# Two up projections computed by Strassen's seven products

## The chip, the cores and the metric

One core of one Trainium2 chip runs the kernel. The metric is device microseconds for one execution. TensorE (PE) multiplies, with its weight loads counted apart (PEld); VectorE (DVE) and ScalarE (ACT) do the elementwise work; SyncE's queue (SP) issues the transfers from HBM.

## The reference

Two residual blocks work on 512 tokens of width 1024, in float32. The first is two layers deep, the second one layer. What the change touches are the parts with the large weight matrices:

```
# first block, twice
proj = u @ w_in[l]                     # 1024 x 5444, then attention, convolution, gates
x = x + merged @ w_mix_out[l]
u = rmsnorm(x, norm_mlp[l])
x = x + square(relu(u @ w_mlp_up[l])) @ w_mlp_down[l]     # 1024 -> 4096 -> 1024
# second block, once
mod = silu(c) @ w_ada + b_ada          # shifts, scales and gates, 1024 x 6144
h = modulate(rms_norm(x, g_ffn), sh_f, sc_f)
x = x + gt_f * ((silu(h @ w_gate) * (h @ w_up)) @ w_down) # 1024 -> 2816 -> 1024
```

## The kernel before

Activations stand transposed: a tile holds 128 features by 512 tokens, so `x` is eight tiles. A product takes a 128x128 piece of the weights as the stationary operand and streams 512 tokens. To keep float32 accuracy with TensorE's rounded float32 type, each operand is split into a high part and a low part (`split` for weights, L171 on ScalarE and L172 on VectorE; `hilo` for activations, L285 and L286), and three matmuls stand for one: high x high, high x low, low x high (L230 to L232 in `linear`). `gateup` has a loop of its own for the FFN (L1315 to L1317).

Weights come in chunks of 1 MB (L161, three buffers). A chunk is cut into units of 4 k-tiles by 256 columns, and each unit is split when the order of work reaches two units ahead of it; four buffers hold split units. The order of work is a list of items that `Prog.run` goes through: a "unit" makes the splits that are due and runs as many background pieces as the rate allows, a "do" emits instructions. A scheduler then orders each engine's queue and places the tiles; a tile of the common pool (60 tiles of 128x512) is free again after its last reader.

In an MLP layer the hidden 4096 features are worked in four groups of 1024. `up` makes eight hidden tiles of one group, four at a time, over eight k-tiles. `evup` evacuates each from PSUM: scale and relu on VectorE (L732), square on ScalarE (L733), then `hilo`. `down` multiplies the group's hidden tiles into all eight output tiles, and `evdn` adds each to `x` (L740). The groups stand one behind the other: up 0, up 1, down 0, up 2, down 1, and so on. In layer 1 the background pieces are `ada`: the 1024 x 6144 matrix is multiplied by a vector on VectorE (L803), 48 steps of two, each with two loads of its own, at 0.8 steps a unit.

The FFN does the same with a pair of matrices: `gateup` makes two gate tiles and two up tiles, applies silu on ScalarE (L1323), multiplies them (L1326) and splits the result (L1330, L1331); `evff` adds the down tiles to `x` (L1345). Where a stage waits for a norm, `parts_=2` runs the tokens in two halves, with matmuls of 256 columns.

Of the kernel before, what the change touches and what calls it, by code (L numbers as in the profile page):

```python
# [17 lines left out]
D = 1024  # L18
NT = T // P
# [6 lines left out]
FF2 = 2816  # L26

# [13 lines left out]
K_RES = 1408  # L41
# [6 lines left out]
class Prog:  # L48


    def __init__(self, split, ahead):
        self.items = []
        self.split = split
        self.ahead = ahead

    def run(self):
        units = [p for k, p in self.items if k == "unit"]
        nxt = 0
# [4 lines left out]
        for kind, pay in self.items:  # L63
            if kind == "unit":
                while nxt < len(units) and nxt <= cur + self.ahead:
                    self.split(units[nxt])
                    nxt += 1
# [32 lines left out]

@with_exitstack
def blocks_kernel(ctx: ExitStack, tc: tile.TileContext, a: dict, out: bass.AP, stop=None):
# [5 lines left out]
    gp = ctx.enter_context(tc.tile_pool(name="gp", bufs=60))  # L108
    bp = ctx.enter_context(tc.tile_pool(name="bp", bufs=1))
    rawp = ctx.enter_context(tc.tile_pool(name="rawp", bufs=3))  # L110
    whp = ctx.enter_context(tc.tile_pool(name="whp", bufs=4))
    sp = ctx.enter_context(tc.tile_pool(name="sp", bufs=4))
# [43 lines left out]
    raws = {}  # L156

    def fetch(chunk):
        W, r0, kt, c0, cw = chunk
        raw = rawp.tile([P, kt, cw], F32, tag="raw", name=nm("raw"))  # L160
        nc.sync.dma_start(raw, W[r0 : r0 + kt * P, c0 : c0 + cw].rearrange("(k p) c -> p k c", p=P))  # L161
        return raw

    def split(u):
        chunk, k0, kn, cc0, ccn = u["src"]
        if id(chunk) not in raws:
            raws[id(chunk)] = fetch(chunk)
        raw = raws[id(chunk)][:, k0 : k0 + kn, cc0 : cc0 + ccn]
        hi = whp.tile([P, kn, ccn], F32R, tag="wh", name=nm("wh"))
        lo = whp.tile([P, kn, ccn], F32R, tag="wl", name=nm("wl"))  # L170
# [4 lines left out]
    prog = Prog(split, 2)  # L175
# [5 lines left out]
    def halves(ch):  # L181

        us = []
        for c in range(0, ch[4], 256):
            us.append({"src": (ch, 0, ch[2], c, min(256, ch[4] - c))})
        return us

    def linear(W, row0, kts, c0, widths, xs, evac, parts_=1):
# [13 lines left out]
        for kt in kts:  # L202
            ch = chunk(W, row0 + kbase * P, kt, c0, cw)
            us = halves(ch)
            steps.append((kbase, kt, us))
            kbase += kt
        for part in range(parts_):
            cs = slice(part * TW, (part + 1) * TW)
            for kbase, kt, us in steps:
                for u in us:  # L210
# [3 lines left out]
                    for j, w in enumerate(widths):  # L214
# [5 lines left out]
                        def emit(u=u, j=j, o=o, w=w, kb=kbase, kt=kt, cs=cs):  # L220
                            if kb == 0:
                                bank[j] = mmbank()
# [14 lines left out]
                        first = False  # L237
        return pieces
# [50 lines left out]
    def prep(key, j, gcol, sq=True):  # L289
# [166 lines left out]
    def dma_in(chunks):  # L456
        def f():
# [9 lines left out]
            for ch in chunks:  # L467
                for _ in range(ch[2]):
                    nc.sync.dma_start(x[j], a["xT"][j * P : (j + 1) * P, :])
                    j += 1  # L470
                raws[id(ch)] = fetch(ch)
# [12 lines left out]
    def layer1(l, nextprep):  # L484
# [25 lines left out]

        def norm():
            rstd("n")
            rs = S["n", "rs"]
            Cr, Sr, rs2 = slot(), slot(), slot()
            dve.tensor_mul(Cr, kon[:, K_RC : K_RC + T], rs)
            dve.tensor_mul(Sr, kon[:, K_RS : K_RS + T], rs)
            S["Cr"], S["Sr"] = Cr, Sr
# [23 lines left out]
        if l == 0:  # L541
            do(dma_in([gC[4 * n][0][1]["src"][0] for n in range(3)] + [gC[12][0][1]["src"][0]]))
            add(gC)
            do(lambda: [square("n", j) for j in range(KT)])
        else:
            add(gC)
# [182 lines left out]
        def evup(c, g):  # L729
            def f(j, ps, cs):  # L730
                r = slot()
                dve.scalar_tensor_tensor(r, ps, 0.0, S["n", "rs"], op0=ALU.max, op1=ALU.mult)  # L732
                S["act"] = act.activation(r, r, AF.Square)  # L733
                hid[c, 4 * g + j] = hilo(r)
            return f

        def evdn(c, g):
            def f(j, ps, cs):
                j = 4 * g + j
                dve.tensor_add(x[j][:, cs], ps, x[j][:, cs])  # L740
                if c == 3:
# [736 lines left out]
```

## Time and profile before

| what | value |
|---|---|
| median of 3 runs (lowest, highest) | 2069.94 us (2069.59, 2069.95) |
| the profiled execution, its span | 2069.96 us, 2067.9 us |
| matmuls recorded, mean DMA rate | 9944, 103 GB/s |
| first MLP, second MLP, FFN in the span | 372 to 737, 1081 to 1416, 1720 to 2060 us |

All durations come from the one profiled execution. A row of a timeline gives start and length in us, the engine, the line, the operation, output and input tiles, shapes and count, and in brackets the idle time before and what ended it. In a group the busy time and the mean ns of one instruction stand behind the bar. Matmuls are pipelined: each is longer than the distance to the next, so their pace is read from starts.

### The profile page before, as it was taken

The numbers are of one execution on the slowest core, as the hardware profiler recorded it, in microseconds if no ns is written. First come the engines' busy times: TensorE is split into PE (matmuls) and PEld (weight loads), VectorE is DVE, ScalarE is ACT, GpSimd is POOL, SyncE is SP. The second block draws the span as 40 slices with busy tenths as digits, with TensorE's granted clock in tenths as the row PEclk, the third lists the DMA queues.
The fourth block names the chain that finished last, engine by engine and source line by source line (L and its number), as shares of the span: only waits on it lengthen the run. The fifth ranks groups of instructions, "written<-read, shape, count | busy, mean of one in ns | idle before, by whom it ended". The sixth has DMA issues, their size and how long they took to land.

```text
span 2067.9 us, 25080 instructions
## 1 busy us (share of the span) xinstructions
PE 2057.1 (99%) x9944; PEld 1700.7 (82%) x9944; DVE 1260.0 (61%) x2245; ACT 845.6 (41%) x1359; POOL 19.7 (1%) x33
## 2 busy tenths in 40 slices
PE   9999999999999999999999999999999999999999
PEld 7888888888888878888888888889877798888887
DVE  6999666644444569977657746567777375333333
ACT  5324773432322332238644322425377744322221
POOL 0000000000000000000000000000010000000000
PEclk9999999999999999999999999999999999999999
DMA  5222213233323222331134545452221123233231
GB/s 204 102 94 93 79 62 102 82 102 102 96 88 102 87 94 90 102 102 62 62 123 169 209 141 194 145 195 98 82 82 62 42 81 103 81 103 101 83 111 51
DMA packets 122148, 215.25 MB, mean 104 GB/s; under 512 B 5808, under 2 KB 30640, under 8 KB 122032
## 3 DMA queue, kind: packets, MB, share of 16 engines
q1 hardware_dynamic: 122032, 213.67, 30.9%
q8 instruction: 78, 1.28, 0.2%
q14 instruction: 38, 0.31, 0.0%
HBM read 211.55 MB, written 2.10 MB: 103 GB/s over the span
## 4 chain that ended last, share of the span: by engine, by line
PE 97%; DVE 1%; ACT 1%; issue 0%; DMA 0%; POOL 0%; SPq 0%; POOLq 0%; DVEq 0%; ACTq 0%
PE mm L230 25%; PE mm L232 25%; PE mm L231 25%; PE mm L1315 4%; PE mm L1317 4%; PE mm L1316 4%; PE at L352 1%; PE mm L260 1%; PE mm L261 1%; PE mm L262 1%; PE ot L386 1%; PE at L371 1%; PE at L1188 0%; PE at L1196 0%; PE at L582 0%
## 5 line engine op out<-in xcount | busy, mean ns | idle before, releaser
L230 PE MATMUL mm<-g,wh 128*128 128x512 f32 (+1 forms) x2400 | 919.5, 384 | 1.0 <-ACT wh L171 0.8
L232 PE MATMUL mm<-g,wl 128*128 128x512 f32 (+1 forms) x2400 | 916.0, 382 | 0.0
L231 PE MATMUL mm<-g,wh 128*128 128x512 f32 (+1 forms) x2400 | 915.4, 382 | 0.0
L171 ACT CAST wh<-raw 128x1024 fp32r<-128x1024 f32 (+2 forms) x356 | 366.4, 1032 | 825.8 <-PE mm L231 648.6
L172 DVE TENSOR_TENSOR wl<-raw,wh 128x1024 fp32r<-128x1024 f32 (+2 forms) x356 | 424.9, 1195 | 448.1 <-ACT wh L171 445.8
L230 PEld LDWEIGHTS mm<-g,wh 128*128 128x128 f32 x2400 | 450.4, 188 | 90.5 <-issue 4.3
L231 PEld LDWEIGHTS mm<-g,wh 128*128 128x128 f32 x2400 | 450.6, 188 | 86.3 <-issue 1.2
L232 PEld LDWEIGHTS mm<-g,wl 128*128 128x128 f32 x2400 | 450.7, 188 | 86.1
L1317 PE MATMUL mm<-g,wl 128*128 128x512 f32 (+1 forms) x384 | 142.6, 372 | 0.0
L1316 PE MATMUL mm<-g,wh 128*128 128x512 f32 (+1 forms) x384 | 142.4, 372 | 0.0
L1315 PE MATMUL mm<-g,wh 128*128 128x512 f32 (+1 forms) x384 | 142.2, 372 | 0.0
L286 DVE TENSOR_TENSOR g<-g,g 128x512 fp32r<-128x512 f32 x96 | 66.4, 691 | 49.7 <-ACT g L285 49.2
L285 ACT CAST g<-g 128x512 fp32r<-128x512 f32 x96 | 59.6, 621 | 60.6 <-DVE g L707 26.6
L1317 PEld LDWEIGHTS mm<-g,wl 128*128 128x128 f32 x384 | 72.3, 188 | 12.6
L1316 PEld LDWEIGHTS mm<-g,wh 128*128 128x128 f32 x384 | 72.3, 188 | 12.5
L1315 PEld LDWEIGHTS mm<-g,wh 128*128 128x128 f32 x384 | 72.1, 188 | 12.4
L740 DVE TENSOR_TENSOR x<-mm,x 128x512 f32<-128x512 f32 (+1 forms) x68 | 44.8, 658 | 56.5 <-PE mm L232 56.5
L803 DVE SCALAR_TENSOR_TENSOR g<-g,g 128x512 f32<-128x512 f32 x96 | 63.8, 688 | 8.6 <-DMA g<-w_ada 8.5
L733 ACT ACTIVATE g<-g 128x512 f32<-128x512 f32 x64 | 40.3, 630 | 70.1 <-DVE g L732 70.1
L360 ACT ACTIVATE g<-g,nm 128x128 f32<-128x128 f32 (+3 forms) x96 | 53.2, 555 | 17.8 <-DVE nm L355 17.1
L601 DVE MAX8 m<-g 128x8 f32<-128x256 f32 (+2 forms) x96 | 53.3, 558 | 1.9
L602 DVE MATCH_REPLACE8 g<-m,g 128x256 f32<-128x256 f32 (+2 forms) x96 | 52.1, 543 | 0.0
(222 smaller groups left out, 1574.4 us busy)
## 6 DMA issues: line engine op xcount, KB each, us to landing
raw<-w_in SPq DMA_DIRECT2D x53, 1024.0 KB, 5.0
raw<-w_mlp_up SPq DMA_DIRECT2D x32, 1024.0 KB, 5.4
raw<-w_mlp_down SPq DMA_DIRECT2D x32, 1024.0 KB, 5.1
g<-w_ada SPq DMA_DIRECT2D x96, 256.0 KB, 5.6
raw<-w_gate SPq DMA_DIRECT2D x11, 1024.0 KB, 5.1
raw<-w_up SPq DMA_DIRECT2D x11, 1024.0 KB, 5.2
raw<-w_down SPq DMA_DIRECT2D x10, 1024.0 KB, 5.0
raw<-w_mix_out SPq DMA_DIRECT2D x8, 1024.0 KB, 5.1
```

The lines of the kernel that those rows point to most:

```text
L171: act.copy(hi, raw)
L172: dve.tensor_sub(lo, raw, hi.bitcast(F32))
L230: pe.matmul(ps, wh, hi[:, cs], start=st, stop=False)
L231: pe.matmul(ps, wh, lo[:, cs], start=False, stop=False)
L232: S["pe"] = pe.matmul(ps, wl, hi[:, cs], start=False, stop=en)
L285: act.copy(hi, src)
L286: dve.tensor_sub(lo, src, hi.bitcast(F32))
L601: dve.max(m8, acc[i][:, :W_])
L803: dve.scalar_tensor_tensor(w, w, 1.0, S["cb", n2], op0=ALU.mult, op1=ALU.mult, accum_out=modp[:, n2, n : n + 1])
L1315: pe.matmul(ps, wh, hi[:, cs], start=s == 0 and k_ == 0, stop=False)
L1316: pe.matmul(ps, wh, lo[:, cs], start=False, stop=False)
L1317: pe.matmul(ps, wl, hi[:, cs], start=False, stop=s == 1 and k_ == 3)
```

## The change

For one block of 1024 x 512 weights the product is written as 2 x 2: the weights are cut into A (`a`, k-tiles 0 to 3, first 256 columns), B (`b`, k-tiles 4 to 7, the same columns), C and D (`c`, `d`, the second 256 columns), the tokens into two halves of 256. Winograd's form of Strassen's method then needs seven products of a 512 x 256 weight matrix with 512 features x 256 tokens, instead of eight. Each product has 4 k-tiles, 2 column tiles and 3 passes, so 24 matmuls of 256 columns. Four of the seven weight matrices are sums, formed by VectorE in float32 and then split as before. Sums of activations (`ta`, `tb`) are made once a stage by `mix`. Sums of outputs are formed in three PSUM banks X, Y and Z: products accumulate on each other, and after the sixth VectorE and ScalarE rewrite Y and Z.

The blocks are the MLP groups of 512 hidden features 1 to 7 of 8 (group 0 stays direct), and the FFN's pairs of 256 gate and 256 up columns 2 to 10 of 11. Between the products the down tiles of the group before are laid (`mesh`); a down now has 4 k-tiles, takes units of 128 columns from the common pool (now 62 tiles) and banks from the pool of the attention. Loads are half MBs, five units ahead, in eight buffers. `ada` runs in both layers, 24 steps each, at 0.25 a unit. The rope tables are loaded into common tiles in each layer.

```diff
+        us = {
+            1: {"load": get("a", "c"), "make": lambda: raw["a"], "post": p1},
+            5: {"load": get("d"), "make": lambda: ws["s"], "post": p5},
+            6: {"make": lambda: ws["s"], "post": p6},
+            2: {"load": get("b"), "make": lambda: raw["b"], "post": p2},
+            7: {"make": lambda: raw["c"]},
+            3: {"make": lambda: ws["s"]},
+            4: {"make": lambda: raw["d"]},
+        }
+        def keep(n, b):
+            def f():
+                tmp[n] = slot()
+                act.copy(tmp[n], bank[b])
+            return f
+        def e6():
+            u = tmp.pop(1)
+            dve.tensor_sub(u, bank["Y"], u)
+            dve.tensor_sub(bank["Z"], bank["Z"], u)
+            act.copy(bank["Y"], u)
+        def e2():
+            evac(0, 0, bank.pop("X"), False)
+        def e7():
+            r = tmp.pop(5)
+            dve.tensor_sub(r, bank["Y"], r)
+            evac(1, 1, r, True)
+        prods = [
+            (1, "X", half(xs, 0, 0), keep(1, "X")),
+            (5, "Z", half(ta, 0, 0), keep(5, "Z")),
+            (6, "Y", half(tb, 0, 0), e6),
+            (2, "X", half(xs, 4, 0), e2),
+            (7, "Y", half(ta, 0, 1), e7),
+            (3, "Z", half(xs, 4, 1), e3),
+            (4, "Y", half(tb, 0, 1), e4),
+        ]
+            piece = [("unit", u)]
+            for m in range(2):
...
+                    ps = bank[b][:, th(m)]
+                    for k in range(4):
+                        pe.matmul(ps, wh, hi, start=first and m == 0 and k == 0, stop=False, skip_group_check=True)
+                        pe.matmul(ps, wh, lo, start=False, stop=False, skip_group_check=True)
+                        S["pe"] = pe.matmul(ps, wl, hi, start=False, stop=k == 3, skip_group_check=True)
...
+    def mix(key, k, y):
+        def first():
+            y0, y1 = y(k), y(k + 4)
+            a_, b_ = st["a"], st["b"] = slot(), slot()
+            dve.tensor_sub(a_[:, th(0)], y0[:, th(0)], y0[:, th(1)])
+            dve.tensor_add(b_[:, th(0)], y1[:, th(1)], a_[:, th(0)])
+            dve.tensor_sub(a_[:, th(1)], y0[:, th(1)], y1[:, th(1)])
+            dve.tensor_sub(b_[:, th(1)], y1[:, th(0)], b_[:, th(0)])
+        def second():
+            S[key, "ta", k] = hilo(st.pop("a"))
+            S[key, "tb", k] = hilo(st.pop("b"))
...
+        def evup(c):
+            def f(n, t, src, own):
+                r = src if own else slot()
+                dve.scalar_tensor_tensor(two(r), two(src), 0.0, both(S["n", "rs"][:, th(t)]), op0=ALU.max, op1=ALU.mult)
                 S["act"] = act.activation(r, r, AF.Square)
+                for m in range(2):
+                    k_ = 4 * c + 2 * n + m
...
+                    act.copy(hi[:, th(t)], r[:, th(m)])
+                    dve.tensor_sub(lo[:, th(t)], r[:, th(m)], hi[:, th(t)].bitcast(F32))
...
+        u0 = linear(W_up, 0, [4, 4], 0, [P] * 4, xs, ev0)
         add(u0[:2])
         do(lambda: rstd("n"))
+        I.append(("rate", 2.5))
+        I.append(("bg", [f for k in range(4) for f in mix("n", k, y)]))
         add(u0[2:])
+        I.append(("drain", None))
+        do(ada_start)
+        I.append(("rate", 0.25))
+        I.append(("bg", [ada(n) for n in range(24 * l, 24 * l + 24)] + ([ada_end] if l else [])))
+        for c in range(1, NU):
+            I.extend(mesh(up(c), down(c - 1)))
...
+        add(down(NU - 1))
...
+        u0 = gateup(0, 2)
+        I.append(("rate", 2.0))
+        I.append(("bg", [f for k in range(4) for f in mix("h", k, y)]))
+        add(gateup(1, 1))
+        I.append(("drain", None))
+        for c in range(2, NG - 1, 2):
+            I.extend(mesh(unit(c) + unit(c + 1), down(c // 2 - 1)))
+        I.extend(mesh(unit(NG - 1), down(ND - 2)))
+        add(down(ND - 1))
```

The table `us` says which matrix each product takes: `p1` forms C + D behind the split of A, `p5` adds A to that sum, `p6` adds A to C, `p2` takes B into the sum (its signs are carried by the output sums). `e3` and `e4` evacuate Z and Y as `e2` does X. The FFN's evacuation applies silu to the gate half and multiplies the up half with it, per token half.

## Rows read from the trace of the kernel before

**Rows 1.** the page's span and busy times (us, share of span, instructions)

```profile
span 2067.9 us, 25080 instructions
...
PE 2057.1 (99%) x9944; PEld 1700.7 (82%) x9944; DVE 1260.0 (61%) x2245; ACT 845.6 (41%) x1359; POOL 19.7 (1%) x33
```

**Rows 2.** the page's chain of waits, shares of the span by engine

```profile
PE 97%; DVE 1%; ACT 1%; issue 0%; DMA 0%; POOL 0%; SPq 0%; POOLq 0%; DVEq 0%; ACTq 0%
```

**Rows 3.** windows, two MLPs and FFN: PE, PEld, DVE, ACT, POOL busy, clock

```profile
372.00:737.00 365.00, 365.00 (x1611) 302.22 (x1610) 161.43 (x183) 121.67 (x154) 0.00 (x0) 1.00 0.29 95
1081.00:1416.00 335.00, 334.95 (x1532) 279.49 (x1530) 208.90 (x372) 115.41 (x147) 0.32 (x1) 1.00 0.50 173
1720.00:2060.00 340.00, 340.00 (x1528) 282.64 (x1527) 119.33 (x132) 88.45 (x108) 0.00 (x0) 1.00 0.27 90
```

**Rows 4.** timeline of PE, 512-column matmuls, first and last of fifteen

```profile
399.82 0.39 PE L232 MATMUL mm<-g,wl 128*128 128x512 f32 x1
...
402.99 0.39 PE L231 MATMUL mm<-g,wh 128*128 128x512 f32 x1
```

**Rows 5.** timeline of PE, 256-column matmuls, first and last of thirty-six

```profile
1404.77 0.28 PE L231 MATMUL mm<-g,wh 128*128 128x256 f32 x1
...
1408.97 0.28 PE L230 MATMUL mm<-g,wh 128*128 128x256 f32 x1
```

**Rows 6.** groups by line and form, PE weight loads (busy us, mean ns)

```profile
L230 PEld LDWEIGHTS mm<-g,wh 128*128 128x128 f32 x2384 | 448.2, 188 | 89.3 <-issue 4.3 <-ACT wh L171 1.2 <-ACT g L860 0.6
```

**Rows 7.** timeline of DVE, three starts in a packed stretch of the second MLP

```profile
1132.22 1.22 DVE L172 TENSOR_TENSOR wl<-raw,wh 128x1024 fp32r<-128x1024 f32 x1
1133.36 0.68 DVE L803 SCALAR_TENSOR_TENSOR g<-g,g 128x512 f32<-128x512 f32 x1
...
1133.97 0.69 DVE L732 SCALAR_TENSOR_TENSOR g<-mm,g 128x512 f32<-128x512 f32 x1
```

**Rows 8.** groups by line and form, DVE

```profile
L172 DVE TENSOR_TENSOR wl<-raw,wh 128x1024 fp32r<-128x1024 f32 x342 | 417.5, 1222 | 436.5 <-ACT wh L171 434.2 <-PE at L313 0.7
...
L732 DVE SCALAR_TENSOR_TENSOR g<-mm,g 128x512 f32<-128x512 f32 x64 | 44.2, 690 | 7.2 <-PE mm L232 7.0
...
L1345 DVE SCALAR_TENSOR_TENSOR x<-mm,modc,x 128x512 f32<-128x512 f32 x24 | 18.0, 751 | 34.7 <-PE mm L232 34.7
...
L317 DVE RECIPROCAL g<-g 128x512 f32<-128x512 f32 x4 | 13.4, 3344 | 0.0
...
L1331 DVE TENSOR_TENSOR g<-g,g 128x256 fp32r<-128x256 f32 x4 | 1.7, 418 | 0.1
```

**Rows 9.** groups by line and form, ACT

```profile
L171 ACT CAST wh<-raw 128x1024 fp32r<-128x1024 f32 x342 | 359.6, 1053 | 802.8 <-PE mm L231 627.4 <-PE mm L1316 81.0 <-issue 71.4
...
L733 ACT ACTIVATE g<-g 128x512 f32<-128x512 f32 x64 | 40.3, 630 | 70.1 <-DVE g L732 70.1
...
L1330 ACT CAST g<-g 128x256 fp32r<-128x256 f32 x4 | 1.6, 406 | 1.7 <-DVE g L1326 1.7
```

**Rows 10.** timeline of ACT in the first MLP, a cast and what follows

```profile
431.98 1.05 ACT L171 CAST wh<-raw 128x1024 fp32r<-128x1024 f32 x1 [0.48 <-PE mm L231]
432.94 0.62 ACT L733 ACTIVATE g<-g 128x512 f32<-128x512 f32 x1
```

**Rows 11.** DMA issues by tile (KB each, median us to landing)

```profile
raw<-w_gate SPq DMA_DIRECT2D x11, 1024.0 KB, 5.1
...
raw<-w_down SPq DMA_DIRECT2D x10, 1024.0 KB, 5.0
...
raw<-w_down SPq DMA_DIRECT2D x2, 512.0 KB, 3.6
```

**Rows 12.** waits in 1081 to 1416 us (us in total, times, longest us)

```profile
DVE g L803 <- DMA g<-w_ada: 8.5, 10, 1.3
```

**Rows 13.** timeline of DVE in the first MLP, two waits for ACT

```profile
431.53 0.69 DVE L286 TENSOR_TENSOR g<-g,g 128x512 fp32r<-128x512 f32 x1 [1.35 <-ACT g L285]
...
433.07 1.23 DVE L172 TENSOR_TENSOR wl<-raw,wh 128x1024 fp32r<-128x1024 f32 x1 [0.17 <-ACT wh L171]
```

More of the change, by code (lines that the diff above doesn't have):

```diff
@@ L18 @@
 D = 1024
+H = T // 2
 NT = T // P
@@ L48, with __init__ @@
 class Prog:
-    def __init__(self, split, ahead):
+    def __init__(self, fetch, split, early, ahead):
         self.items = []
+        self.fetch = fetch
         self.split = split
+        self.early = early
         self.ahead = ahead
@@ L64, in run @@
             if kind == "unit":
+                while got < len(units) and got <= cur + self.early:
+                    self.fetch(units[got])
+                    got += 1
                 while nxt < len(units) and nxt <= cur + self.ahead:
@@ L98, in interleave, with mesh @@
     return out
+def mesh(a, b):
+    n = len(a)
+    out = []
+    for i, x in enumerate(a):
+        out.extend(x)
+        for p in b[i * len(b) // n : (i + 1) * len(b) // n]:
+            out.extend(p)
+    return out
 @with_exitstack
@@ L162, in fetch, with granule @@
         return raw
-    def split(u):
[L165 to L170, printed above, removed]
+    def granule(u):
+        ch, k0, kn, cc0, ccn = u["src"]
+        W, r0, kt, c0, cw = ch
+        if kt * cw <= GRAN:
+            return (id(ch), 0, 0), (W, r0, kt, c0, cw)
+        gw = min(max(ccn, GRAN // kn), cw - cc0 // (GRAN // kn) * (GRAN // kn))
+        g0 = cc0 // (GRAN // kn) * (GRAN // kn)
+        return (id(ch), k0, g0), (W, r0 + k0 * P, kn, c0 + g0, gw)
+    def fetch(u):
+        if "load" in u:
+            u["load"]()
+        if "src" in u:
+            key, what = granule(u)
+            if key not in raws:
+                raws[key] = load(*what)
+    def split(u):
+        if "make" in u:
+            raw = u["make"]()
+            kn, ccn = raw.shape[1:]
+        else:
+            ch, k0, kn, cc0, ccn = u["src"]
+            key, what = granule(u)
+            k0, cc0 = (k0, cc0) if key[1:] == (0, 0) and what[2] * what[4] == ch[2] * ch[4] else (0, cc0 - key[2])
+            raw = raws[key][:, k0 : k0 + kn, cc0 : cc0 + ccn]
+        if u.get("narrow"):
+            hi, lo = (slot(F32R, kn * ccn).rearrange("p (k c) -> p k c", k=kn) for _ in range(2))
+        else:
+            hi = whp.tile([P, kn, ccn], F32R, tag="wh", name=nm("wh"))
+            lo = whp.tile([P, kn, ccn], F32R, tag="wl", name=nm("wl"))
         act.copy(hi, raw)
@@ L179, in chunk, with halves, linear @@
         return [W, r0, kt, c0, cw]
-    def halves(ch):
+    def halves(ch, narrow):
         us = []
-        for c in range(0, ch[4], 256):
-            us.append({"src": (ch, 0, ch[2], c, min(256, ch[4] - c))})
+        uw = P if narrow else 256
+        for c in range(0, ch[4], uw):
+            us.append({"src": (ch, 0, ch[2], c, min(uw, ch[4] - c)), "narrow": narrow})
         return us
-    def linear(W, row0, kts, c0, widths, xs, evac, parts_=1):
+    def linear(W, row0, kts, c0, widths, xs, evac, parts_=1, narrow=False, newbank=mmbank):
         pieces = []
@@ L541, in layer1 @@
         if l == 0:
-            do(dma_in([gC[4 * n][0][1]["src"][0] for n in range(3)] + [gC[12][0][1]["src"][0]]))
+            do(dma_in([[p[0][1] for p in gC[4 * n : 4 * n + 4] if p[0][0] == "unit"] for n in range(4)]))
+            do(rope_tables)
             add(gC)
```

220 lines of the change are left out of this document (151 added, 69 removed).

## The prediction

> **What bounds the kernel now.** I read the busy shares first. TensorE is busy 2057.1 of 2067.9 us and VectorE 1260.0 [rows 1], so 10.8 us of the span are without a matmul. Then the chain of waits: 97% of it is TensorE, 1% each VectorE and ScalarE [rows 2]. Then the three stages that the change rewrites, by windows: the two MLPs and the FFN show TensorE busy without a gap, with VectorE at 44%, 62% and 35% [rows 3]. [...] In these stages only fewer or cheaper matmuls shorten the kernel; everything else costs nothing until it makes TensorE wait. The profiled execution took 2069.96 us, 2.06 us more than its span, and stands at the median of the runs (2069.94); I sum against it.
>
> **The products.** One block of the old up or gate/up path (4 output tiles, 8 k-tiles, 3 passes) is 96 matmuls of 512 columns. Consecutive starts are 0.2264 us apart: 399.82 to 402.99 is 14 steps [rows 4]. That is 96 x 0.2264 = 21.73 us. The same block as seven products is 7 x 2 x 4 x 3 = 168 matmuls of 256 columns. That form stands in the trace too, in the last down tiles of layer 1, which run in two halves: 1404.77 to 1408.97 is 35 steps, 0.1200 us each [rows 5]. 168 x 0.1200 = 20.16 us. So seven products instead of eight give not an eighth (2.72 us) but 1.57 us, because two short matmuls take 0.2400 and one long takes 0.2264. A weight load of 188 ns [rows 6] stands beside each matmul in both stretches, so the closer loading is already in the 0.1200. In numbers of columns: (226.4 - 120.0)/256 = 0.416 ns a column, and 13.6 ns per matmul whatever its width. Strassen pays that 13.6 ns 72 times more.
>
> [...]
>
> How many blocks: in each MLP 7 of the 8 groups of four tiles (the first stays direct), in the FFN units 2 to 10, nine. 14 + 9 = 23, and 23 x 1.57 = **36.2 us** less TensorE. The down tiles keep their matmuls and widths; the direct remainder too.
>
> **VectorE, in the MLP.** A seven-block needs 7 split weights where four stood, 4 weight sums, 2 + 1 output sums, 4 evacuations. One pair, block plus one down of 8 tiles, lasts 20.16 + 21.73 = 41.9 us on TensorE. Packed instructions start a little closer than their length: a 128x1024 subtraction at 1132.22 is followed at 1133.36 (1.14 us), the 512-wide instruction that follows by the next at 1133.97 (0.61) [rows 7]. With these steps, and the forms in [rows 8]: splits 7 x 1.14 = 8.0; narrow down splits 8 x 0.61 = 4.9; sums 4 x 1.14 = 4.6; output sums 3 x 0.61 = 1.8; evacuation 4 x 0.61 + 8 low parts of 256 columns at 0.42 = 5.8; x updates 8 x 0.61 = 4.9; together 30.0. The ada rows now run in both layers, one step of two multiplications per four units, 15 units a pair, so 3.75 x 2 x 0.69 = 5.2. In all 35.2 of 41.9 us, 84%, where the layer with ada had 62%. With whole lengths (1.22 for 1.14, 0.69 for 0.61) it is 37.9. VectorE stays below TensorE by either, but with little to spare. In the FFN, two blocks and one down last 62.1 us. VectorE has 8.0 + 4.6 + 1.8 + 2 x 0.61 + 4 x 0.42 = 17.3 a block and 4.9 + 8 x 0.75 = 10.9 a down, so 45.5, 73%. No row shows a VectorE sum written into PSUM (Z minus u): bounds 0.42 and 1.22 us; I take 0.69, the length of its neighbours that read PSUM [rows 8], and it is hidden in the same reserve.
>
> **ScalarE:** 7 x 1.05 + 8 x 0.63 + 3 copies x 0.63 + 4 x 0.63 + 8 x 0.41 = 20.1 us of 41.9 [rows 9]. No bound.
>
> **Waits inside a block.** Product 7 accumulates on what the step after product 6 leaves in Y: one subtraction, one copy, 0.69 + 0.63 us, with at most one 1.22 and one 1.05 us instruction ahead of them, 3.6 us. Between the two products lie a product of 2.88 us and one to three down tiles of 2.72 us, so 5.6 us at least (FFN) and 11 us in the MLP. Product 4 waits for one subtraction of 0.69 us behind product 7, with 5.6 us between. The other banks have longer. Behind a late product the whole TensorE queue stands. Splits have lead: the cast at 431.98 was released by a matmul, the last reader of its slot, and stands ahead of the activation at 432.94 that belongs to the unit just ended [rows 10]; with four slots that is a cast four units early. Four wide slots now serve only products, so they reach further in time; the narrow down units take general slots and reach two units, 5.6 us, for a cast and a subtraction of 1.3 us. I put 0.1 us per block, **+2 us** in all (bounds 0 and 1 us a block, 23, by the 1.05 to 1.22 us of one instruction in the way).
>
> **Openings.** Each MLP must build the mixed inputs while the first four tiles run. From their start VectorE has: the norm 3.34 + 4 x 0.61 = 5.8 (its reciprocal is the 3.34 [rows 8]); mixing 4 x (4 x 0.42 + 2 x 0.61) = 11.6; four evacuations of two instructions 4.9; the last split of the group 1.14; then, for products 1 and 5 and the first down tile, 3 x 1.14 + 0.61 = 4.0. Sum 27.4 us. Product 5, the first that needs a mixed input, comes at 21.7 + 2.9 + 2.7 = 27.3 us. That fits only if VectorE hardly waits and had part of it done before; ScalarE supplies every mix first. I charge 1.5 us twice, **+3** (bounds 0 and 6 each: the whole mix late by half). In the FFN mixing also adds high and low back together, 4 x 2 x 0.61 = 4.9 more, but VectorE was two thirds idle there [rows 3]: **+1** (0 to 5).
>
> **Seams.** The last down starts 2.72 us after the last product and needs its result for k-tiles 2 and 3 only, 1.36 us later: 4.1 us for a chain of 0.69 + 0.63 + 0.41 + 0.42 = 2.2 us. Nothing (0 to 1.5, three times).
>
> **Loads.** Bytes are the same; half-MB loads land in 3.6 us against 5.0 for 1 MB, and rows of 1 KB (w_gate, 5.1) land as fast as rows of 2 KB (w_down) [rows 11]. Eight buffers of half a MB hold more than three of 1 MB, and the seven products keep four of them. SP's issues double and each waits for its buffer; a late one would hold those of ada behind it. The rope tables move from the constants to slots, same bytes in layer 0, 0.5 MB more in layer 1. Nothing, -3 to +3 us (the 10.8 us without a matmul are what could be gained).
>
> **Sum:** 2069.96 - 36.2 + 2 + 3 + 1 = **2039.8 us**.
>
> **Rivals.**
> A. Stalls eat up to two thirds: the ada rows hold VectorE. At 84% load a VectorE queue that stands at an ada row for its DMA delays the splits behind it. For: there were 10 such waits, 8.5 us in all, with a longest of 1.3 us [rows 12]. Against: TensorE then lost only 0.05 us [rows 3]. If each of the 48 steps cost 0.3 us, 14 us more: about 2054, in a band of 2046 to 2064.
> B. No change: every block loses what it gains, 1.57 us, at one place, most likely product 7 waiting for the copy into Y. For: the FFN's 5.6 us against a 3.6 us chain. Against: 11 us in the MLP. 2066 to 2074.
> C. Slower: VectorE becomes the bound in the MLPs. With whole lengths it has 37.9 us a pair; the old pair took 2 x 21.73 = 43.5. 23 subtractions of a pair follow a ScalarE result; if VectorE stands 0.24 us at each, the pair takes 43.5 and the MLPs gain nothing. The trace has such waits of 0.17 to 1.35 us [rows 13], though at times when VectorE had nothing else to do. At 0.4 us: 37.9 + 9.2 = 47.1 us, 14 x 3.6 = 50 us over before, less the FFN's 9 x 1.57 = 14: about 2106. It decides from VectorE's busy share near 95% in the MLP windows. Against: before the change, stretches where VectorE ran packed made TensorE wait for 0.05 us in the MLP windows [rows 3].
> D. The change gains more: the 13.6 ns per matmul is not paid by the products. Both widths then lose it, 96 x 212.8 - 168 x 106.4 ns = 2.55 us a block, 58.7 in all, 2017. The rows speak against. [...]
> That the change does not do what it says would show as 512-column matmuls left in the up path; the diff leaves no room.
>
> **How the numbers follow.** Forecast (2030 to 2046): 0.62. A 0.16, B 0.06, C 0.14, D 0.02. Less than 0.2% (4.1 us) is not to be told from no change here. Faster: 0.62 + 0.16 + 0.02 = 0.80; the same 0.05, most of B; slower 0.15, C and a rest of B. The range 2030 to 2064 holds the forecast's case and A, 0.78 and a little; the upper end leaves B and C out.
>
> **What would show it.** Products: 256-column matmuls 0.120 us apart, 168 a block, a pair in 41.9 us. VectorE: 80 to 90% busy in the MLP windows and about 73% in the FFN. Stalls: idle TensorE after the first four tiles of each MLP, ended by VectorE on a mixed input; almost none elsewhere. It would be wrong if VectorE or a PSUM bank ends repeated gaps in the middle of the stages, or if the short matmuls don't hold 0.120 us in company of a dense VectorE.

## The result and the profile after

The kernel after the change takes 2082.49 us (median of 4 runs, 2081.03 to 2084.37) against 2069.87 for the kernel before on the same chip: ratio 1.0062 [1.0044, 1.0079], 12.6 us slower. The forecast was 2039.8, range 2030 to 2064. The profiled execution took 2082.21 us.

The page of the kernel after, span, busy times and chain by engine, against [rows 1, 2]:

```profile
span 2079.9 us, 29624 instructions
...
PE 2041.5 (98%) x11552; PEld 1759.0 (85%) x11552; DVE 1575.5 (76%) x2801; ACT 982.9 (47%) x1699; POOL 19.5 (1%) x33
...
PE 91%; DVE 6%; ACT 2%; issue 1%; DMA 0%; POOL 0%; SPq 0%; DVEq 0%; ACTq 0%; POOLq 0%
```

TensorE is now without a matmul for 38.4 us of the span, where it was 10.8, and VectorE is 6% of the chain, where it was 1%. Busy TensorE fell by 15.6 us, less than the 36.2 forecast, for the most part because its mean granted clock fell from 1.000 to 0.991: 0.9% of 2080 is, as an estimate, up to 19 us of matmuls running longer. The rest is a smaller gain of the products (below).

To see where, I took as markers between stages the matmuls that sum the squares for a norm (512 columns wide up to layer 1's MLP, one column wide from layer 1's last down on); "products gain" is what the prediction expected:

| stage | before, us | after, us | products gain | so lost |
|---|---|---|---|---|
| layer 0, MLP up to the next mixer's norm | 368.10 | 371.16 | 7 x 1.57 = 11.0 | 14.1 |
| layer 1, mixer | 340.91 | 340.56 | | -0.35 |
| layer 1, MLP into its last down tiles | 335.26 | 341.70 | 11.0 | 17.4 |
| norm behind them and second block's mixer | 275.31 | 280.28 | | 5.0 |
| FFN to the last matmul | 372.71 | 370.67 | 9 x 1.57 = 14.1 | 12.1 |

The third and fourth rows after are worked out from 347.46 and 274.52: the second half of the last down tiles, on which the marker hangs, was 11.5 us long before and is 5.8 us after, so 5.76 us moved from one stage to the other. The losses come to 48.3 us, against the 36.2 gained: 12.1 us, the difference of the two spans (12.0) within 0.1.

The middle of each stage is without waits, as forecast. Windows there (columns as in [rows 3]: from and to, length, then busy time of PE, PEld, DVE, ACT and POOL with counts, clock, DMA share, GB/s):

```profile
460.00:660.00 200.00, 200.00 (x1255) 181.26 (x1254) 164.53 (x274) 86.06 (x143) 0.00 (x0) 1.00 0.44 143
1150.00:1350.00 200.00, 200.00 (x1257) 181.39 (x1256) 165.25 (x274) 87.71 (x145) 0.00 (x0) 1.00 0.47 153
1800.00:2030.00 230.00, 230.00 (x1594) 215.25 (x1594) 169.53 (x210) 98.94 (x151) 0.00 (x0) 1.00 0.32 100
```

TensorE has no gap, the clock is 1.00, and VectorE stands at 82%, 83% and 74%. And the timeline of TensorE, the answer to [rows 4, 5], one product and one down tile:

```profile
522.43 0.28 PE L401 MATMUL mm<-g,wh 128*128 128x256 f32 x1
...
525.18 0.28 PE L403 MATMUL mm<-g,wl 128*128 128x256 f32 x1
525.30 0.40 PE L279 MATMUL at<-g,g 128*128 128x512 f32 x1
...
528.05 0.28 PE L401 MATMUL mm<-g,wh 128*128 128x256 f32 x1
```

24 short matmuls from 522.43 to 525.30 are 0.1196 us each, as forecast; the 12 long ones of a down tile take 2.75 us, where 12 x 0.2264 is 2.72. A whole pair, from product 1 to the next product 1 (485.98 to 528.05), takes 42.07 us. Two direct blocks of the kernel before take 2 x 21.73 = 43.46, so a block gains 1.39 us here and not 1.57; in the FFN two blocks and a down take 62.24 us (1836.32 to 1898.56) against 3 x 21.73 = 65.19, 1.48 a block. The 23 blocks gain 14 x 1.39 + 9 x 1.48 = 32.8 us, 3.4 less than the table counts, and its three losses with products shrink to 12.8, 16.2 and 11.3.

So most of the loss is at the openings. The waits of TensorE over the whole span (us in total, times, longest us):

```profile
PE mm L401 <- DVE g L928: 12.6, 4, 4.1
PE mm L1533 <- ACT g L217: 6.7, 3, 4.6
PE at L1056 <- DVE g L1054: 3.3, 3, 1.9
PE mm L401 <- ACT g L354: 2.3, 1, 2.3
...
PE mm L279 <- ACT g L1076: 1.6, 1, 1.6
```

The largest, in TensorE's timeline at the opening of layer 0's MLP (the idle time before the instruction and what ended it in brackets):

```profile
392.82 0.36 PE L401 MATMUL mm<-g,wh 128*128 128x256 f32 x1 [4.06 <-DVE g L928]
...
400.31 0.39 PE L402 MATMUL mm<-g,wh 128*128 128x256 f32 x1 [0.62 <-DVE g L456]
...
403.07 0.39 PE L401 MATMUL mm<-g,wh 128*128 128x256 f32 x1 [2.26 <-DVE g L928]
...
407.03 0.80 PE L279 MATMUL at<-g,g 128*128 128x512 f32 x1 [0.69 <-ACT g L455]
```

L928 is the evacuation of a tile of the direct group (max with 0 and times the norm's factor), which frees its PSUM bank. Product 1 needs such a bank. The first direct tile is complete at about 385 (371.4 and five pieces of 2.72 us), yet VectorE evacuates it only at 392.00. VectorE's timeline shows what it did in between:

```profile
386.38 1.22 DVE L218 TENSOR_TENSOR wl<-ws,wh 128x1024 fp32r<-128x1024 f32 x1
387.51 0.68 DVE L456 TENSOR_TENSOR g<-g,g 128x512 fp32r<-128x512 f32 x1
388.12 1.22 DVE L336 TENSOR_TENSOR ws<-ws,raw 128x1024 f32<-128x1024 f32 x1
389.25 0.68 DVE L456 TENSOR_TENSOR g<-g,g 128x512 fp32r<-128x512 f32 x1
389.86 1.21 DVE L218 TENSOR_TENSOR wl<-raw,wh 128x1024 fp32r<-128x1024 f32 x1
390.99 0.41 DVE L476 TENSOR_TENSOR g<-g 128x256 f32<-128x256 f32 x1
...
392.00 0.68 DVE L928 SCALAR_TENSOR_TENSOR g<-mm,g 128x512 f32<-128x512 f32 x1
```

The reader is to see a queue in a fixed order: the low parts of mixed inputs (L456), a sum for a later product (L336), splits of later weights (L218) and the mixing itself (L476 to L479) all stand ahead of the evacuation for which TensorE waits. Once evacuated, a direct tile goes to ScalarE for its square (L929) and its high part (L455) and back to VectorE for its low part (L456), and VectorE stands still until it comes:

```profile
392.71 0.63 ACT L929 ACTIVATE g<-g 128x512 f32<-128x512 f32 x1 [1.81 <-DVE g L928]
393.37 0.62 ACT L455 CAST g<-g 128x512 fp32r<-128x512 f32 x1
```

```profile
394.03 0.69 DVE L456 TENSOR_TENSOR g<-g,g 128x512 fp32r<-128x512 f32 x1 [1.02 <-ACT g L455]
```

All four direct tiles show this wait (at 394.03, 396.67, 404.37 and 407.00), 5.1 us in all. The wait at 403.07 is for another bank, evacuated at 402.33 behind the next four instructions of mixing (400.77 to 402.00). The MLP of layer 1 shows the same waits (4.06, 0.40, 2.27 and 0.69 us), and one of 2.27 us for ScalarE's copy of a bank (L354) at 1128.35.

Around the waits the clock is lower: it was 1.00 in the three windows without waits above, and is 0.50 to 0.95 in these, of both openings, of the FFN's, and of single stretches in the first:

```profile
371.00:411.00 40.00, 32.37 (x145) 26.47 (x144) 31.24 (x47) 23.04 (x34) 0.00 (x0) 0.87 0.21 69
1083.00:1123.00 40.00, 32.48 (x140) 26.36 (x139) 30.65 (x46) 22.04 (x32) 0.00 (x0) 0.84 0.21 68
1705.00:1770.00 65.00, 57.53 (x368) 51.52 (x367) 55.31 (x117) 30.61 (x59) 0.00 (x0) 0.95 0.23 72
...
390.00:395.00 5.00, 2.18 (x13) 2.21 (x14) 3.98 (x8) 2.16 (x4) 0.00 (x0) 0.85 0.33 108
395.00:400.00 5.00, 4.68 (x26) 4.21 (x25) 3.19 (x5) 4.43 (x8) 0.00 (x0) 0.81 0.00 0
...
405.00:410.00 5.00, 4.31 (x13) 3.05 (x13) 3.54 (x7) 3.29 (x6) 0.00 (x0) 0.50 0.14 55
```

In 40 us of the first opening 7.6 us are idle and 13% of the clock, by estimate some 5 us, is lost. Behind the wait of 4.06 us, from 393.71 to 396.48, the clock is 0.50 and the short matmuls start 0.213 us apart, where they hold 0.1196 at 1.00. From 405 to 410 the clock is 0.50 too, behind the wait at 403.07 and across the one at 407.03. VectorE is 78% busy in the 40 us: it is late without being full, and the four waits for ScalarE are most of its idle time.

The FFN's opening waits 4.63 us at 1725.80 for ScalarE's cast of a weight (L217, 128 columns wide). The modulated norm behind layer 1's last down tiles holds TensorE three times, 4.4 us in all:

```profile
1435.97 0.70 PE L1056 MATMUL at<-g,kon 128*128 128x256 f32 x2 [0.91 <-DVE g L1054]
1438.27 1.22 PE L279 MATMUL mm<-g,wh 128*128 128x256 f32 x4 [1.60 <-ACT g L1076]
1448.41 1.19 PE L1056 MATMUL at<-g,kon 128*128 128x256 f32 x2 [1.89 <-DVE g L1054]
```

The kernel before had two waits there, of 1.18 (1435.05) and 0.17 us.

### The profile page after: what moved, and what is told of

It reads as the page before. It is cut to its first block, busy times and chain, and to the rows that moved or that the text cites. A ratio compares the mean times of both kernels' runs of the same rounds, so it can differ in the third digit from the quotient of the medians.

```text
span 2079.9 us, 29624 instructions
## 1 busy us (share of the span) xinstructions
PE 2041.5 (98%) x11552; PEld 1759.0 (85%) x11552; DVE 1575.5 (76%) x2801; ACT 982.9 (47%) x1699; POOL 19.5 (1%) x33
## 3 DMA queue, kind: packets, MB, share of 16 engines
q1 hardware_dynamic: 198880, 214.73, 32.8%
## 4 chain that ended last, share of the span: by engine, by line
PE 91%; DVE 6%; ACT 2%; issue 1%; DMA 0%; POOL 0%; SPq 0%; DVEq 0%; ACTq 0%; POOLq 0%
PE mm L279 13%; PE mm L280 13%; PE mm L281 13%; PE mm L401 7%; PE mm L402 7%; PE mm L403 7%; PE at L279 7%; PE at L280 7%; PE at L281 7%; PE at L540 1%; PE ot L574 1%; PE mm L430 1%; PE mm L431 1%; PE mm L432 1%; PE at L559 1%
## 5 line engine op out<-in xcount | busy, mean ns | idle before, releaser
L217 ACT CAST wh<-raw 128x1024 fp32r<-128x1024 f32 (+3 forms) x272 | 277.5, 1024 | 537.0 <-PE mm L280 220.1
L279 PE MATMUL mm<-g,wh 128*128 128x512 f32 (+2 forms) x1328 | 506.9, 383 | 2.4 <-ACT g L1076 1.6
L281 PE MATMUL mm<-g,wl 128*128 128x512 f32 (+2 forms) x1328 | 503.4, 379 | 0.0
L280 PE MATMUL mm<-g,wh 128*128 128x512 f32 (+2 forms) x1328 | 502.4, 379 | 0.0
L218 DVE TENSOR_TENSOR wl<-raw,wh 128x1024 fp32r<-128x1024 f32 (+3 forms) x272 | 321.6, 1184 | 128.5 <-ACT wh L217 127.2
L401 PE MATMUL mm<-g,wh 128*128 128x256 f32 x1288 | 367.7, 285 | 14.9 <-DVE g L928 12.6
L402 PE MATMUL mm<-g,wh 128*128 128x256 f32 x1288 | 367.4, 285 | 1.0 <-DVE g L456 1.0
L403 PE MATMUL mm<-g,wl 128*128 128x256 f32 x1288 | 367.3, 285 | 0.0
L279 PEld LDWEIGHTS mm<-g,wh 128*128 128x128 f32 (+1 forms) x1328 | 250.1, 189 | 51.8 <-issue 4.3
L280 PEld LDWEIGHTS mm<-g,wh 128*128 128x128 f32 (+1 forms) x1328 | 250.1, 188 | 45.7 <-issue 1.2
L401 PEld LDWEIGHTS mm<-g,wh 128*128 128x128 f32 x1288 | 250.1, 194 | 22.4 <-issue 8.9
L402 PEld LDWEIGHTS mm<-g,wh 128*128 128x128 f32 x1288 | 249.6, 194 | 7.0 <-DVE g L456 1.4
L279 PE MATMUL at<-g,g 128*128 128x512 f32 x608 | 239.7, 394 | 1.4 <-ACT g L455 1.4
L280 PE MATMUL at<-g,g 128*128 128x512 f32 x608 | 239.5, 394 | 0.1
L281 PE MATMUL at<-g,g 128*128 128x512 f32 x608 | 237.7, 391 | 0.0
L217 ACT CAST wh<-ws 128x1024 fp32r<-128x1024 f32 x69 | 72.4, 1050 | 216.0 <-PE mm L402 205.2
L281 PEld LDWEIGHTS at<-g,g 128*128 128x128 f32 x608 | 114.7, 189 | 24.8
L279 PEld LDWEIGHTS at<-g,g 128*128 128x128 f32 x608 | 115.2, 189 | 22.4 <-ACT g L455 3.0
L280 PEld LDWEIGHTS at<-g,g 128*128 128x128 f32 x608 | 115.2, 190 | 19.5 <-DVE g L456 0.9
L218 DVE TENSOR_TENSOR wl<-ws,wh 128x1024 fp32r<-128x1024 f32 x69 | 84.4, 1223 | 60.6 <-ACT wh L217 60.6
```

The lines of the kernel that those rows point to most:

```text
L279: pe.matmul(ps, wh, hi[:, cs], start=st, stop=False)
L280: pe.matmul(ps, wh, lo[:, cs], start=False, stop=False)
L281: S["pe"] = pe.matmul(ps, wl, hi[:, cs], start=False, stop=en)
L401: pe.matmul(ps, wh, hi, start=first and m == 0 and k == 0, stop=False, skip_group_check=True)
L402: pe.matmul(ps, wh, lo, start=False, stop=False, skip_group_check=True)
L403: S["pe"] = pe.matmul(ps, wl, hi, start=False, stop=k == 3, skip_group_check=True)
```

## The experiments

Ratios are against the kernel before, run on the same chip. The theory after the result: the opening's VectorE queue (a backlog of mixing, splits and sums) keeps TensorE waiting. Its rivals: too few PSUM banks; the clock, which falls first and makes the rest late; VectorE too slow altogether.

**1. Other banks for the first two direct tiles.** They take theirs from the attention's pool, so that product 1 finds a free one.

```diff
-        u0 = linear(W_up, 0, [4, 4], 0, [P] * 4, xs, ev0)
+        b0 = iter([atbank, atbank, mmbank, mmbank])
+        u0 = linear(W_up, 0, [4, 4], 0, [P] * 4, xs, ev0, newbank=lambda: next(b0)())
```

> The first two tiles of each MLP's direct group take banks of the attention pool, so product 1 finds a free bank. Bank theory (the waits of 4.06 and 2.3 us on an evacuation are the loss, because all four banks are held): each MLP opens 6 to 12 us earlier, 2060 to 2070 us. Backlog theory (VectorE's queue is late with everything at the opening): product 1 starts early but the first down tile, which needs the last evacuated hidden tile, still starts at about 36 us after the norm; the wait moves and the time stays, 2079 to 2084.

2075.99 us (2075.67 to 2079.4), ratio 1.0032 [1.0019, 1.0045]: 6.5 us less than with the change alone. The 4.06 us wait went, and another came 4.6 us later, on the first down tile: its weights' cast stands on ScalarE at 396.72, behind the squares and casts of the direct tiles, which wait for VectorE's evacuations:

```profile
397.38 0.80 PE L279 MATMUL at<-g,g 128*128 128x512 f32 x1 [4.88 <-ACT g L217]
```

It fits neither theory in full: between the markers the two MLPs take 2.9 and 4.0 us less, so the bank is worth 3 to 4 us an opening, and the rest of the backlog stays.

**2. No mixing.** The products read the plain inputs in place of the mixed ones, and the sums and splits that mix them are left out, ScalarE's part of them (scaled copies and casts) too.

```diff
         def first():
-            y0, y1 = y(k), y(k + 4)
...
-            dve.tensor_sub(b_[:, th(1)], y1[:, th(0)], b_[:, th(0)])
+            pass
 
         def second():
-            S[key, "ta", k] = hilo(st.pop("a"))
-            S[key, "tb", k] = hilo(st.pop("b"))
+            S[key, "ta", k] = S[key, k]
+            S[key, "tb", k] = S[key, k + 4]
```

> The mixed inputs are not formed; the products that take them read the plain activations (this leaves the sums of activations out of the computation). Backlog theory: 11.6 us of VectorE go from each MLP opening and 16.5 from the FFN's; both MLP openings close, some 14 us each with the clock, the FFN gains 0 to 3: 2050 to 2058. Bank theory (the splits for later products stand ahead of the evacuation and hold the banks, with or without the mix): about half, 2066 to 2072.

2051.23 us, ratio 0.9909 [0.9892, 0.9925]: 31.3 us less. The windows of the two openings, without a wait and at full clock, in the same place as the first two of the windows above:

```profile
371.00:411.00 40.00, 39.93 (x220) 34.43 (x219) 31.53 (x42) 22.11 (x30) 0.00 (x0) 1.00 0.36 117
1070.00:1110.00 40.00, 39.93 (x219) 34.41 (x218) 31.75 (x42) 22.20 (x30) 0.00 (x0) 1.00 0.41 129
```

VectorE is as busy as before, on later work. Between the markers the two MLPs take 12.9 and 16.3 us less, about all that their openings lost, and the FFN 3.0 less. So the MLP openings' loss comes with the mixing: with the same banks and the same products, but without it, there is no wait. Whether VectorE's or ScalarE's part of the mixing does it is not told apart here (experiment 10). What is left, the wait of 4.6 us in the FFN's opening and the 4.4 us at the end of layer 1, has other causes: experiments 5 and 6.

**3. Two direct groups.** Group 1 of each MLP stays direct too, and the mixing is spread over it and the first down tiles. In this kernel the mixing reads x after the first down has added to it, so that this part of the computation is changed.

```diff
+        u1 = linear(W_up, 0, [4, 4], 512, [P] * 4, xs, evd)
...
+        add(u1[:4])
+        I.append(("rate", 1.0))
+        I.append(("bg", [f for k in range(4) for f in mix("n", k, y)]))
+        I.extend(mesh(u1[4:], down(0)))
...
-        for c in range(1, NU):
+        for c in range(2, NU):
...
```

> Groups 0 and 1 of each MLP stay direct and the mixing is spread over group 1 and the first down. It gives back 2 x 1.57 = 3 us of the products. Backlog theory: the openings close for most part, 2082.5 - 24 + 3 = about 2061 (2056 to 2068). If the mixing at the opening is not the cause: 2085.

2055.96 us, ratio 0.9932 [0.9917, 0.9946], at the lower edge of the expected band; the waits of the MLP openings are gone. Against experiment 2 it is 4.7 us more. Between the markers 2.3 of that are in the two MLPs, where two blocks fewer take back 2 x 1.39 = 2.8, and 3.1 in the FFN, whose mixing experiment 2 left out too. The MLPs' whole mix is there, so VectorE has the time for it, if not in one group's 21.7 us.

**4. TensorE kept busy.** Forty matmuls that nobody reads, 40 x 0.12 = 4.8 us, where the 4.06 us wait was. They are to tell the theory from the rival of the clock: the clock was 0.85 and 0.81 in the two windows from 390 to 400, and 1.00 in the windows without waits.

```diff
+        def fill():
+            w = atbank()
+            h = S["n", 0][0]
+            for _ in range(40):
+                pe.matmul(w[:, :H], h[:, :P], h[:, :H], start=True, stop=True)
+
+        do(fill)
```

> 40 matmuls of 256 columns without a reader stand between the direct group and product 1 of each MLP, 4.8 us of work where TensorE waits 4.06 us. [...] Backlog theory (TensorE waits for VectorE until the first down tile at either clock): the same within 2 us, 2080 to 2085.

2081.3 us, ratio 1.0054 [1.0039, 1.0069]; with the change alone 1.0062 [1.0044, 1.0079], the same. The windows and the two later waits:

```profile
390.00:395.00 5.00, 5.00 (x44) 5.00 (x44) 3.98 (x8) 2.06 (x4) 0.00 (x0) 1.00 0.33 105
395.00:400.00 5.00, 3.56 (x24) 2.85 (x23) 3.40 (x6) 4.72 (x8) 0.00 (x0) 1.00 0.02 7
...
405.00:410.00 5.00, 4.31 (x14) 3.16 (x15) 3.54 (x6) 3.29 (x6) 0.00 (x0) 0.50 0.00 2
```

```profile
402.77 0.38 PE L401 MATMUL mm<-g,wh 128*128 128x256 f32 x1 [1.95 <-DVE g L928]
...
406.72 0.79 PE L279 MATMUL at<-g,g 128*128 128x512 f32 x1 [0.69 <-ACT g L455]
```

The clock is 1.00 up to 400, where it was 0.85 and 0.81, but the same two instructions start 0.3 us earlier and no more (403.07 and 407.03 with the change alone). VectorE sets those times. The lower clock came with the waits and is not what made TensorE late up to there; the fall to 0.50 from 405 to 410 stayed.

**5. The first FFN group's weights in wide units.** Two 128-column units become one of 256 columns, split ahead.

```diff
-                (w, s, j): {"src": (ch, 4 * s, 4, P * j, P), "narrow": True}
...
+                    if nparts == 2:
+                        us[w, s, 0] = us[w, s, 1] = {"src": (ch, 4 * s, 4, 0, 256)}
...
```

> Only the FFN's first group, which runs in two token halves, gets units of 256 columns back. Cover theory: a narrow unit hides 1.44 us of splitting per half tile and its split comes behind the norm, so TensorE waits 4.62 us for a cast and then runs slow for some us; with wide units, split ahead of the norm, 6 to 9 us are gained, 2073 to 2077. Rival (the norm on VectorE is the late one, as in the wait of 0.53 us before it): the wait moves to the norm, 2080 to 2083.

2078.4 us, ratio 1.004 [1.0025, 1.0055]: 4.1 us less (3.1 of them in the FFN, between the markers), a smaller gain than expected. The wait of 4.63 us went; behind it stood one of 1.11 us for the norm before the FFN (L1054 at 1722.86), and L217 makes TensorE wait 3.6 us later in the opening, where it was 2.1. So part of the gain wandered on to the next waits.

**6. A longer last down.** In layer 1 the last half of the down tiles takes the k-tiles of groups 6 and 7, eight as before the change, so that the second half of its tokens, which covers the norm, is 11.5 us long again.

```diff
...
+            add(downg(NU - 1, 0))
+            add(linear(a["w_mlp_down"][l], 512 * (NU - 2), [4, 4], 512, [P] * 4, lambda k: hid[4 * (NU - 2) + k],
+                       evdn(NU - 1, 1), parts_=2))
...
```

> In layer 1 the second half of the last down runs over eight k-tiles again (groups 6 and 7 together), so the second token half again covers the final norm of the first with 11.5 us of matmuls instead of 5.8. Cover theory: the waits of 0.91, 1.60 and 1.89 us and the low clock behind them go but for the 1.1 us of before: 5 us gained, 2076 to 2079. Rival (VectorE is late there for other work): no change, 2081 to 2084.

2077.82 us (2075.84 to 2078.71), ratio 1.0034 [1.0022, 1.0047]: 4.7 us less, about the 5.0 of the table. Between 1400 and 1460 there is one wait of 1.17 us and one of 0.17, as in the kernel before, and from the norm's marker to the next it takes 275.29 us (275.31 before the change).

**7. All of it together.** Two direct groups, the mixing spread over five units and finished before the first down; wide first FFN group; longer last down.

```diff
...
-        I.append(("rate", 2.5))
+        I.append(("rate", 1.6))
         I.append(("bg", [f for k in range(4) for f in mix("n", k, y)]))
         add(u0[2:])
+        add(u1[:4])
         I.append(("drain", None))
+        I.extend(mesh(u1[4:], down(0)))
...
```

> Two direct groups with the mixing spread over five units, the wide first FFN group and the longer last down together. Backlog and cover theory: the four openings are the whole loss; 2056 for the first, less 7, less 5: 2044 (2040 to 2050), 1.2% faster than before. If the losses are not independent, or wander to a next wait: 2050 to 2060.

2047.47 us, ratio 0.9889 [0.9874, 0.9904], span 2045.2, clock 1.000: 35.0 us less than with the change alone, inside the expected band. Left in the FFN's opening are 3.6 us of waits for L217 and 1.11 for the norm.

**8. The same with direct products.** The order of experiment 7, but its 21 blocks as eight products of 512 columns.

```diff
-            return seven([(W_up, 512 * c), (W_up, 512 * c + 256)], xs, lambda k: S["n", "ta", k], lambda k: S["n", "tb", k], evup(c))
...
+            return linear(W_up, 0, [4, 4], 512 * c, [P] * 4, xs, ev)
...
```

> As the kernel with all three repairs, but direct products in place of the seven, in the same order with the same loads, units and mixing; 12 blocks in the MLPs and 9 in the FFN. If the products are worth what the steps of 0.2264 and 0.1200 us say, 21 x 1.57 = 33 us more than with them: about 2077. If the order, the half-MB loads and the narrow units cost or give something of their own, the total stands off 2070 by that plus the mixing's waits; if the seven carry waits inside the stages, the difference is smaller than 33.

2074.37 us, ratio 1.0022 [1.0012, 1.0031]. Seven products are worth 26.9 us in this order, less than the 33.0 expected (21 x 1.57). At the pace of the pairs above it would be 12 x 1.39 + 9 x 1.48 = 30.0. In the two MLPs they gave 17.6 us between the markers, where 12 x 1.39 is 16.7. From the last norm's marker to the end it is 375.77 against 366.97 us, 8.8 where nine blocks give 13.3: what is missing lies in the FFN, where experiment 7 waits 3.6 us for L217 and this run 1.3.

**9. A third direct group in the FFN.** Experiment 7 with the FFN's mixing spread over groups 1 and 2, and units 3 to 10 as seven products.

```diff
-        I.append(("rate", 2.0))
+        I.append(("rate", 0.5))
         I.append(("bg", [f for k in range(4) for f in mix("h", k, y)]))
         add(gateup(1, 1))
+        add(gateup(2, 1))
         I.append(("drain", None))
...
+        for c in range(3, NG, 2):
+            I.extend(mesh(unit(c) + unit(c + 1), down((c - 3) // 2)))
...
```

> The kernel with all three repairs, and in the FFN too a further direct group: units 3 to 10 as seven products instead of 2 to 10, the mixing spread over groups 1 and 2. It gives back 1.57 us of products, and the last two downs lose their partner. Backlog theory: the 3.6 us of waits and what VectorE at 95% costs in the FFN's opening go, 2043 to 2046. Rival (the FFN's opening waits for the norm, not for the mixing): 2048 to 2050.

2041.69 us (2041.33 to 2041.86), ratio 0.9862 [0.9845, 0.9878], the best here, 28.3 us faster than the kernel before, and a little better than expected. One block fewer and 5.8 us gained. Its page, and its openings:

```profile
span 2039.8 us, 29213 instructions
...
PE 2029.2 (99%) x11384; PEld 1742.5 (85%) x11384; DVE 1542.5 (76%) x2755; ACT 969.1 (48%) x1669; POOL 19.5 (1%) x33
```

```profile
371.00:411.00 40.00, 39.75 (x173) 31.82 (x171) 34.09 (x49) 24.68 (x35) 0.00 (x0) 1.00 0.23 68
1705.00:1770.00 65.00, 64.95 (x353) 56.31 (x353) 49.84 (x77) 27.96 (x47) 0.00 (x0) 1.00 0.30 91
```

TensorE has 10.6 us without a matmul, as before the change (10.8). Against the kernel before, its 20 blocks come to 28.3 / 20 = 1.41 us each; the pace of the pairs gives 12 x 1.39 + 8 x 1.48 = 28.5 in all, so next to nothing is lost any more. Against the direct products of experiment 8 they are 32.7 us, 1.63 each, but the FFN of that run is 3.1 us slower than that of the kernel before and the two orders differ by one FFN group.

**10. The mixing's sums on GpSimd.** With the change as it is, the four half-wide sums of each mix move from VectorE to GpSimd.

```diff
-            dve.tensor_sub(a_[:, th(0)], y0[:, th(0)], y0[:, th(1)])
...
+            po = nc.gpsimd
+            po.tensor_sub(a_[:, th(0)], y0[:, th(0)], y0[:, th(1)])
...
```

> The changed kernel with the four half-wide sums of each mixing step on GpSimd instead of VectorE: 16 x 0.42 = 6.7 us of the 11.6 leave VectorE at each MLP opening. Backlog theory: the loss falls by about that share, 2062 to 2072. If GpSimd is slow in them the mixed inputs come later still, and the wait moves to the products that read them: 2080 or more.

2076.82 us, ratio 1.0032 [1.0019, 1.0045]: 5.7 us less, a miss in all. By stages it is two effects: between the markers the MLPs take 6.3 and 5.8 us less, as the backlog theory has it (6.7 us of VectorE's work each, with ScalarE's part of the mixing left in place), and the FFN takes 6.2 us more. GpSimd's timeline and the groups of VectorE from 371 to 412, where the change alone had 686 ns for L456 and 1217 for this form of L218:

```profile
375.53 0.74 POOL L477 TENSOR_TENSOR g<-g 128x256 f32<-128x256 f32 x1 [109.31 <-ACT g L981]
...
396.34 1.87 POOL L477 TENSOR_TENSOR g<-g 128x256 f32<-128x256 f32 x1 [4.54 <-ACT g L981]
```

```profile
L456 DVE TENSOR_TENSOR g<-g,g 128x512 fp32r<-128x512 f32 x12 | 8.7, 746 | 4.2 <-ACT g L455 4.2
L218 DVE TENSOR_TENSOR wl<-ws,wh 128x1024 fp32r<-128x1024 f32 x3 | 4.2, 1398 | 1.2 <-ACT wh L217 1.2
```

The same sum takes 0.74 to 1.87 us on GpSimd, and the means of VectorE's two groups grow by 9% and 15% (of the three L218 one took 1.76 us). The long waits at 392.82 and 403.07 went (what is left there is at most 1.04 us each), but the FFN's opening now waits 11.0 us for casts (L217), where it was 6.7.

## Why the prediction was wrong

**The products: right in kind, 3.4 us too large.** 1.57 us a block was worked out from 0.2264 and 0.1200, and the short matmuls hold 0.1196. But a down tile between products takes 2.75 us and not 2.72, which the sum did not have, and a pair takes 42.07 us (forecast 41.9): 1.39 us a block in the MLPs, 1.48 in the FFN, 32.8 in all instead of 36.2. Experiment 9 agrees with 1.41.

**VectorE in the steady state: right.** 84% and 73% were forecast, 82%, 83% and 74% measured. The sum into PSUM, of which no row told, took 696 ns (forecast 0.69):

```profile
L360 DVE TENSOR_TENSOR mm<-mm,g 128x512 f32<-128x512 f32 x23 | 16.0, 696 | 0.3
```

**Waits inside a block: right.** 2 us were charged. The three windows in the middle of the stages have none; one of 2.27 us (1128.35, for ScalarE's copy of a bank, L354) stands in layer 1's first block, behind the opening.

**Openings: the step that failed.** The prediction charged 3 us for the two MLPs and 1 for the FFN, with upper bounds of 6 for each MLP and 5 for the FFN. By the table they cost 14.1, 17.4 and 12.1; with the products at their measured gain 12.8, 16.2 and 11.3. Three things were wrong in the working:
- It set VectorE's work, 27.4 us, against 27.3 us of TensorE, said itself that this fits only if VectorE hardly waits, and charged 1.5 us an opening all the same. It named ScalarE as the supplier of the mixes; what VectorE waited for most was ScalarE's part in the evacuation of the direct tiles, 5.1 us at L456, and 3.1 us more at the low parts of weights (L218, for the casts of L217). With the 5.1 alone the work is late for any deadline at 27.3. The same wait, 1.35 us, stands in [rows 13] at 431.53; rival C read it as time in which VectorE had nothing else to do, and in the opening VectorE had.
- It took product 5 as the first to need anything late. The mixed input that it looked at made TensorE wait 0.62 us (L456 at 400.31). Its sign named the place, behind the first four tiles, but a mixed input as what ends the wait. The first to wait was product 1, right behind the direct group, for the bank of a direct tile whose evacuation stood behind mixes and later splits. A sum of work tells nothing of an instruction's place in a queue.
- The bound, the whole mix late by half, counted the wait only and had no term for the clock: in [rows 3] TensorE had no gap and the clock was 1.00. It was 0.87, 0.84 and 0.95 in the three windows, by estimate from them 5, 6 and 3 us of TensorE's time. Not all of that adds to the waits: in experiment 4 the clock stayed at 1.00 up to 400 and TensorE was 0.3 us earlier. How much of the rest adds is not shown.

**The FFN's opening: weights that the prediction did not look at.** "The direct remainder" kept its matmuls, as the prediction said. But its 128-column units now have to be split two ahead, with 1.4 us of matmuls each in the first group's halves, behind the norm on ScalarE, and cost the 4.63 us wait (experiment 5: 4.1 us). Without the mixing (experiment 2) the FFN takes 3.0 us less. Both repairs with the mixing spread over one more direct group (experiment 9) leave 0.7 of the 11.3 us; how these parts share the rest is not shown.

**Seams: "nothing" left out the end of layer 1.** The forecast followed the product's chain into the last down. What it missed is that the last down has half the k-tiles, so that the work that hides the norm behind it shrank from 11.5 to 5.8 us: 5.0 us, shown by experiment 6 (4.7). Together the openings (36.3 more than charged), the products (3.4) and this seam, less the 2 us charged within the blocks and 0.35 gained in layer 1's mixer, come to 42.4 us, as much as the profiled execution took beyond the forecast (2082.21 against 2039.8).

**Loads: nothing,** as charged; no wait of TensorE names a DMA.

**The rivals.** A had the size of a stall case (2046 to 2064), but its place, the ada rows in the steady state, does not occur: the windows there are full. B and C fall: no repeated gaps in the middle of the stages and no stretch there where VectorE sets the pace. D falls: the short matmuls stand 0.1196 us apart, where 0.1064 would be left without the 13.6 ns that the forecast worked out from [rows 4, 5]. (D's 2017 holds the 6 us of charged waits.) What came true lies on rival C's side, slower, by a mechanism that the prediction had as a small term of its likeliest case.

Still open: why the seven products gave 4.5 us less in the FFN of experiment 7 than their pace (2.3 us are waits for L217); why the order of experiment 8 is 4.4 us slower than the kernel before with the same products (3.1 of them in the FFN); and how much of the clock's loss after 405, left by experiment 4, would stay with the last wait alone, which wasn't tried.

## What to carry to other kernels

Cost the opening of a stage by the order of its queues: list for the first consumer what stands ahead of its producer on that engine, with the waits on the engine that feeds it, and don't set a sum of work against a deadline alone. When a change shortens a piece of work, look for what that piece was hiding. A change that is right in the steady state and slower in all can be cured by keeping the old form for one more group, so that the preparation spreads: here 20 blocks in place of 23, with two smaller repairs, gave 28 us in place of a loss of 13.

## What the runs showed of the hardware that was not expected

Around waits of 2.3 us (403.07) and 0.7 us (407.03), TensorE's granted clock was 0.50 from 405 to 410; with 4.8 us of readerless matmuls ahead of it (experiment 4) the clock was 1.00 until 400 and 0.50 again from 405 to 410, around the same waits (1.95 and 0.69 us).

In experiment 10 some of GpSimd's sums, and some instructions of VectorE, took longer while the other engine worked. A half-wide sum took 0.73 us at 384.62, where VectorE stood idle (384.05 to 385.34), and 0.74 or 0.75 four times from 375.53 to 378.49. At 381.90 it took 1.60 us, beside a split of VectorE (L218 at 381.15) that took 1.76 us, where this form had a mean of 1.217 with the change alone. At 387.09 VectorE's low part of a mixed input (L456) took 1.24 us beside sums of 1.07 and 1.06, against a mean of 0.686. Not every instruction of VectorE grew: the split at 388.85 took 1.21 us beside a sum of 1.78. What tells the two cases apart is not shown.
